# The second query-key product over all 128 rows of TensorE, with a zero-padded query tile

## The chip, the cores and the metric

One NeuronCore of a Trainium2 chip runs the whole program. The metric is the device time of one launch in microseconds (us), lower is better. TensorE does the matmuls (PE in the profile, with PEld for its weight loads), VectorE is DVE, ScalarE is ACT, GpSimd is POOL, and SP issues the DMAs. A matmul here takes a weight tile of at most 128 rows (the contracted dimension, on the partitions) by 128 columns, and streams up to 512 columns of the other operand past it into a bank of PSUM.

## What is computed

One inference step of a single transformer layer for 1024 prompt tokens and 64 sample tokens, width 1024, all in fp32. Cut to what matters here:

```python
h = pre(x, g_pre_mix, shift1, scale1)                  # RMSNorm, then conditioning
qd, kd, vd, qs, ks, vs = split_proj(h @ w_in)
# 4 heads of differential attention, two maps of 64 features each
s = einsum('bqhmd,bkhmd->bhmqk', qd, kd) * 64 ** -0.5 - slopes * dist
p = softmax(where(visible, s, NEG)); a = p[:, :, 0] - lam * p[:, :, 1]
od = rmsnorm(a @ vd) * (1 - lam_init)
# 8 heads of stick-breaking attention of 64 features each
z = einsum('bqhd,bkhd->bhqk', qs, ks) * 64 ** -0.5
w = where(earlier, exp(log_sigmoid(z) + between), 0); osb = w @ vs
x = x + gate1 * rmsnorm(concat(od, osb) @ w_out)
x = x + gate2 * rmsnorm(relu(h2 @ w_up) ** 2 @ w_down)
```

The sample's 64 queries attend to 1024 cached keys and their own 64.

## The kernel before

TensorE reads a reduced fp32 form, so every operand is held as an exact sum of a high and a low part (`split`), and a product is the sum of three partial products, high-high, high-low and low-high.

**Stages.** Up to about 55 us the conditioning vectors and the first tokens are prepared. From there to about 745 us attention runs, with the input projections of the eight units mixed in. Then come the output projection (to about 820 us) and the feed-forward part, a long row of matmuls (lines 299 to 301 and 1117 to 1120) up to the end.

**Units and steps.** There are eight units `u`: 0 to 3 are the differential heads, 4 to 7 are pairs of stick-breaking heads. A unit has two halves of 64 features, its two maps or its two heads, on partitions 0 to 63 and 64 to 127. The class `Diff` makes a step of one query tile `t` of 128 queries and both maps; `Stick` makes a step of two query tiles, 2q and 2q + 1, and one head `hd`; `Sample` is the sample's step. Each step has a `score` part (query-key products and the weights from them), an `apply` part (the weights transposed on TensorE, line 572, and multiplied with the values, lines 588 and 589 or 737 and 738) and a `finish` part. The main loop runs `apply` of step j and `score` of step j + 1 alternately, and between them the `Filler` puts pieces of the next unit's projections (lines 299 to 301), so many per piece of attention that each token group is done when a step needs it: the list `need` holds these due steps.

**The product that is touched.** `qk` (line 557) makes one block of up to 512 scores in two matmuls into one PSUM bank. Per half `m`, the tile `Q[m]` holds the high part of the queries on the half's own 64 partitions and the low part on the other 64, and `Kd[m]` holds the high part of the keys twice. So line 561 contracts over 128 rows and gives high-high plus low-high in one go. Line 562 adds the queries' high part times the keys' low part `Kl`; it contracts over the half's 64 rows only:

```python
mm(ps[:, :w], lhsT=S["Q"][m][:, qt], rhs=S["Kd"][m][:, c0 : c0 + w], start=True, stop=False)
mm(ps[:, :w], lhsT=S["Q"][m][r, qt], rhs=S["Kl"][r, c0 : c0 + w], start=False, stop=True)
```

A `Diff` step's scores go to DVE (line 641, minimum) and ACT (line 610, exponential), a `Stick` step's to ACT (lines 716 and 717, two sigmoids), POOL (line 701, the triangular mask) and DVE (lines 693 and 694, running product and weights).

**Order and buffers.** The order on each engine comes from the framework's scheduler, which starts from the order in which the code is written. Each engine takes its instructions strictly in that order. Tiles of one tag share a fixed number of buffers: tag `h` (6 buffers) holds the projections' input parts, later those of the output projection and of the feed-forward part, and at the end the tiles `xy` of the last sums.

Of the kernel before, what the change touches and what calls it, by code (L numbers as in the profile page):

```python
# [34 lines left out]
def build(tc, I, O):  # L35
# [9 lines left out]
    BUFS = dict(h=6, w=6, raw=3, qk=10, v=2, s=11)  # L45
# [16 lines left out]
    def split(src, hi, lo, eh=None, el=None):  # L62
        """src = hi + lo exactly, both in FP32r."""
        (eh or nc.scalar.copy)(hi, src)  # L64
        (el or nc.vector).tensor_tensor(lo, src, fr(hi), ALU.subtract)  # L65
# [4 lines left out]
    # ------------------------------------------------------------- constants  # L70
# [21 lines left out]
    # ---------------------------------------------------------------- x load  # L92
# [9 lines left out]

    def group_tiles(name):
        return [[big(f"{name}{c}{g}", "h", [P, KT, 384]) for c in "hl"] for g in range(3)]
# [11 lines left out]
    # conditioning vectors, gains and biases of adaLN: rows to be transposed into columns  # L116
# [64 lines left out]
    # --------------------------------------------------------- adaLN columns  # L181
    gD = dr.tile([2, 2, D], F32, name="gD")

    def ada_rows(c0, name, ps=None, between=()):
        """silu(c) @ w_ada for 256 columns from c0, prompt's and sample's in rows 32j and 32j + 1: four summands in TensorE's four
        column tiles, the rows between them 0."""
        if ps is None:
            ps = bank("pa" + name, "pj")[:, :256]
        for q in range(2):
            raw = ada_raws.get((c0, q))  # L190
            if raw is None:
                raw = big(f"ar{name}{q}", "raw", [P, 4, 256], F32)
                load(raw, w_ada[:, 4 * q : 4 * q + 4, c0 : c0 + 256])
            if q == 1 and between:
                between.pop()()
            for i in range(4):
                mm(ps[32 * i : 32 * i + 32], lhsT=sc[:, 4 * q + i, :], rhs=raw[:, i, :], start=(q == 0), stop=(q == 1), skip_group_check=True)
            yield 0.5
        return ps

    def sum_to_columns(R, n, name):
        """Rows' summands added, features on the partitions: [128, feature block, prompt | sample]."""
        ps = bank(name, "pj")
        for i in range(n):
            mm(ps[:, 2 * i : 2 * i + 2], lhsT=R[:, i * P : (i + 1) * P], rhs=sel, start=True, stop=True)
        return ps[:, 0 : 2 * n].rearrange("p (k j) -> p k j", j=2)

    def modulation(first, cols, name):
        """Columns A = (1 + scale) * gain and B = shift."""
# [21 lines left out]
    def gate_rows(first, gpost, name, slot, tags):  # L231
        """(gate + bias) * gain by conditioning vector, to DRAM."""
# [22 lines left out]
    def split_T(x, half, dst, m, rows):  # L255
        """Half of the token tile's transposed rows into its group's parts; the sample's also side by side (hi | lo)."""
# [7 lines left out]
    def modulated(ps, half, m, A, B, dst, name):  # L264
        """One half of the features, from the transposed normalised rows to the group's parts."""
# [28 lines left out]
    def dense_T(ps, w, act, g, ks=range(KT)):  # L294
        """ps[128 output features, the group's tokens]; yields its cost by and by."""
# [19 lines left out]
    def columns(ps, q):  # L315
        """Columns 2q, 2q+1 of A = (1 + scale) * gain and B = shift, from rows [shift | scale]."""
# [9 lines left out]
    def block_T(g, k, tag):  # L326
        """Feature block k of the group's normalised tokens, features on the partitions."""
# [25 lines left out]
    def first(k):  # L353
        """Block k's part of the first group's products."""
        for i in range(3):
            drain(dense_T(PS[i], PW[0, i], hT, 0, (k,)))
# [46 lines left out]
    # lambda  # L403
# [11 lines left out]
    # per row: 1 for the first map's queries, -lambda for the second's  # L415
# [4 lines left out]
    # ---------------------------------------------------------- projections  # L420
# [6 lines left out]
    for i in range(2):  # L427
        nc.scalar.copy(bd[:, i, :], zero)

# [8 lines left out]
    def natural(f, u, g, out, name):  # L438
        """Tokens back onto partitions, and to the output."""
# [91 lines left out]
    def proj(u, g):  # L531
        for i, f in enumerate((proj_q, proj_k, proj_v)):
            if (u, i) not in PW:
                PW[u, i] = proj_weights(u, i)
            for n, c in enumerate(f(u, g, PW[u, i])):
                yield c
                # the next group gets ready meanwhile
# [14 lines left out]

    # --------------------------------------------- attention, step by step
    # A step has parts `score` (products with the keys, and the weights from them), `apply` (weights transposed, times the
    # values) and `finish` (to the mixed features); `finish` and the next step's `score` run between parts of `apply`.

    def qk(u, m, t, c0, w, name):
        S = U[u]
        ps = bank(name, "qk")
        r, qt = slice(64 * m, 64 * m + 64), slice(P * t, P * t + P)  # L560
        mm(ps[:, :w], lhsT=S["Q"][m][:, qt], rhs=S["Kd"][m][:, c0 : c0 + w], start=True, stop=False)  # L561
        mm(ps[:, :w], lhsT=S["Q"][m][r, qt], rhs=S["Kl"][r, c0 : c0 + w], start=False, stop=True)  # L562
# [5 lines left out]
    def transposed(srcs, name, kr=P):  # L568
        """[rows, 128] blocks to [128, rows] side by side, in two parts."""
# [8 lines left out]
    def apply_rows(po, parts, values):  # L578
        """Weights' rows on output partitions: po[rows, value hi | lo] over blocks of (group, its weights' sources, rows)."""
# [27 lines left out]
    def exp_rows(e, mn, l):  # L607
        """e = exp(-e + mn) per chunk, their sum in l[:, 0:1]."""
# [12 lines left out]
    class Diff:  # L621
        def __init__(self, u, t):
            self.u, self.t, self.name = u, t, f"{u}_{t}"
            self.cost = 0.33 * (t + 1) + 0.8 * (1 + t // 4) + 0.1

# [60 lines left out]
    def stick(s, kp):  # L686
        """Chunks in place: kp = sigmoid(-z) becomes its product over this and all later keys, s = sigmoid(z) the weights
        (the very last key's s is 0 in every row)."""
# [9 lines left out]
    def earlier(s, kp, n):  # L698
        """Only keys before the query: [rows, n] with row and key counted from the same position."""
# [3 lines left out]
    class Stick:  # L703
        def __init__(self, u, q, hd):
            self.u, self.q, self.hd, self.name = u, q, hd, f"{u}_{q}{hd}"
            self.cost = 0.22 * (4 * q + 3) + 0.43 * (q + 1) + 0.1

# [56 lines left out]
    # the sample's: queries of two maps (or heads) on the partitions, keys of the cache and then the new ones  # L764
# [4 lines left out]
    class Sample:  # L769
        def __init__(self, u):  # L770
            self.u, self.name, self.cost = u, f"S{u}", 6.3

# [112 lines left out]
    class Filler:  # L885
        """Work for TensorE between the steps' dependent parts."""
# [35 lines left out]
    def merge(a, b):  # L922
        """a's parts with b's between them."""
# [22 lines left out]
    for u in range(8):  # L946
        sec = [st for st in sections[u] if not isinstance(st, Sample)]
        for st, g in zip((sec[0], sec[3], sec[6]) if u < 4 else (sec[0], sec[2], sec[6]), range(3)):
# [10 lines left out]
    def some(rows, n):  # L959
        """The next n chunks of adaLN's rows."""  # L960
# [9 lines left out]
    for u in range(8):  # L970
        for g in range(3):
            if u + g:
                fill.add(proj(u, g), 12, (u, g))
            if g == (2) and u in others:
                gen, n, c = others[u]
                fill.add(some(gen, n), c, "end" if u == 7 else None)
    drain(steps[0].score())
    prev = None
    for j, st in enumerate(steps):
# [4 lines left out]
        ratio = max([fill.cost_to(mark) / sum(cost[j : i - 1]) for i, mark in need if i > j + 1 and sum(cost[j : i - 1]) > 0] + [0.0])  # L984
        for c in merge(st.apply(), nxt.score() if nxt is not None else ()):
# [8 lines left out]
    # ------------------------------------------------------------ out_proj  # L994
# [18 lines left out]
    def tail_T(m, xn):  # L1013
        g = m // 3
        if h2[g] is None:
            h2[g] = [big(f"h2{c}{g}", "h", [P, KT, 384]) for c in "hl"]
        modulated_T(xn, m, A2, B2, h2, f"b{m}")

    for m in range(NTT):
# [24 lines left out]
        # x' = x + gate * gain * rmsnorm, and its rows over their root mean square  # L1044
# [13 lines left out]
    # ---------------------------------------------------------------- FFN  # L1058
# [49 lines left out]
    def down(b, m, blocks, then=None):  # L1108
        """Adds hidden blocks (parts of the hidden tiles, weights) to the token tile's sum."""
# [21 lines left out]
    def last_down(b, m, blocks, G):  # L1131
        """The token tile's last blocks, then out = x + G * rmsnorm(sum)."""
# [76 lines left out]
def constants():  # L1209
    """Arrays that depend on shapes alone: ALiBi distances with the chunk mask, and selectors."""  # L1210
# [31 lines left out]
```

## Time and profile before

| | us |
|---|---|
| median of 3 runs | 1632.2 (1627.46 to 1635.94) |
| profiled execution, first to last instruction (its own time is not listed apart from this span) | 1633.9 |
| up to the first scores | 55 |
| differential units, settled | 120 to 400 |
| stick-breaking units | 400 to 680 |
| last unit's attention, its projections done | 680 to 745 |
| output projection | 745 to 820 |
| feed-forward part | 820 to 1634 |

Of the views, the page gives the busy time of each engine over the whole span, and the chain of work that ended last: from the last instruction back to what released it, step by step, so that an engine's share of the chain is the share of the span that it set. A matmul's record runs from its start to a modelled end, and successive matmuls overlap; what one costs in a row of matmuls is the distance from its start to the next one's start. A weight load that begins while the matmul before still runs is hidden. The windows view gives busy times for stretches of the span, with the granted clock of TensorE as a share of 2.4 GHz.

### The profile page before, as it was taken

The page shows a single profiled execution, that of the slowest core. Times are in us where ns is not written, and L with a number is a line of the kernel's source. Part 1 is how long each engine was busy: PE and PEld are TensorE (multiplying, and loading weights), DVE is VectorE, ACT ScalarE, POOL GpSimd, SP SyncE. Part 2 cuts the span into 40 slices and gives each one's busy share as a digit, 9 for nine tenths or more (in the row PEclk, how much of TensorE's full clock was granted, in tenths as well). Part 3 has the DMA queues.
Part 4 walks back from the last instruction along what each step waited for, and adds up shares of the span by engine and source line. Part 5 has one row for each costly group of instructions (what it writes and reads, how often), then busy time and mean ns, then how long its engine had stood idle before and what let it go on. Part 6 is the DMA issues. An engine that isn't in the chain of part 4 may idle for free.

```text
span 1633.9 us, 23611 instructions
## 1 busy us (share of the span) xinstructions
PE 1582.2 (97%) x8682; PEld 1364.0 (83%) x8682; DVE 981.2 (60%) x1880; ACT 707.2 (43%) x1661; POOL 330.3 (20%) x516
## 2 busy tenths in 40 slices
PE   6999999999999999978999999999999999999998
PEld 4779887878797988757889899889989989998996
DVE  3675667676878788797554344454454455445447
ACT  3756666666655656664665312122111212211122
POOL 0442333333433242253211000000000000000002
PEclk9799999999998999778999999999999999999999
DMA  9312124232313120346321201222111111111124
GB/s 320 87 49 86 59 80 119 82 113 74 113 50 114 47 87 20 95 133 205 128 80 60 75 19 62 78 79 62 41 32 47 40 52 52 51 40 34 45 90 161
DMA packets 152517, 133.21 MB, mean 82 GB/s; under 512 B 11233, under 2 KB 136274, under 8 KB 152402
## 3 DMA queue, kind: packets, MB, share of 16 engines
q1 hardware_dynamic: 152402, 131.71, 25.9%
q8 instruction: 68, 1.11, 0.3%
q14 instruction: 47, 0.39, 0.1%
HBM read 108.59 MB, written 23.09 MB: 81 GB/s over the span
## 4 chain that ended last, share of the span: by engine, by line
PE 83%; DVE 7%; issue 3%; ACT 1%; POOL 1%; DMA 1%; POOLq 0%; DVEq 0%; ACTq 0%
PE pu L300 8%; PE pu L299 8%; PE pu L301 8%; PE pd L1117 7%; PE pd L1118 7%; PE pd L1120 6%; PE pz L562 4%; PE pt L572 2%; PE pz L561 2%; DVE k L693 2%; PE pq L299 2%; PE py L1032 2%; PE pk L299 2%; PE py L1031 2%; PE pq L300 2%
## 5 line engine op out<-in xcount | busy, mean ns | idle before, releaser
L1124 DVE TENSOR_TENSOR acc<-pd,acc 128x512 f32<-128x512 f32 x252 | 171.0, 687 | 112.2 <-PE pd L1120 105.9
L1102 ACT ACTIVATE sq<-pu 128x384 f32<-128x384 f32 (+1 forms) x96 | 45.3, 472 | 315.1 <-PE pu L301 315.1
L1103 DVE TENSOR_TENSOR sq<-sq 128x384 f32<-128x384 f32 (+1 forms) x96 | 72.0, 750 | 178.4 <-ACT sq L1102 178.4
L562 PE MATMUL pz<-Kl,Q 64*128 64x512 f32 (+2 forms) x192 | 88.9, 463 | 0.0
L65 DVE TENSOR_TENSOR al<-pt,ah 128x512 fp32r<-128x512 f32 (+2 forms) x128 | 75.8, 599 | 19.7 <-ACT ah L64 18.1
L64 ACT CAST ah<-pt 128x512 fp32r<-128x512 f32 (+2 forms) x128 | 65.0, 521 | 39.2 <-PE pt L572 29.6
L561 PE MATMUL pz<-K,Q 128*128 128x512 f32 (+2 forms) x192 | 77.8, 406 | 2.1 <-ACT K L498 1.2
L572 PE MATMUL pt<-ident,s 128*128 128x128 f32 x432 | 74.1, 289 | 3.1 <-DVE s L663 2.6
L610 ACT ACTIVATE s<-s,mn 128x512 f32<-128x512 f32 (+3 forms) x96 | 58.5, 611 | 37.1 <-DVE mn L641 34.8
L562 PEld LDWEIGHTS pz<-Kl,Q 64*128 64x128 f32 x192 | 37.1, 193 | 42.6 <-issue 36.8
L693 DVE TENSOR_TENSOR_SCAN k<-k 128x127 f32<-128x127 f32 (+3 forms) x64 | 56.0, 878 | 13.3 <-POOL k L701 12.6
L716 ACT ACTIVATE s<-pz 128x512 f32<-128x512 f32 (+2 forms) x96 | 47.5, 495 | 34.4 <-PE pz L562 25.2
L694 DVE TENSOR_TENSOR s<-s,k 128x127 f32<-128x127 f32 (+3 forms) x96 | 60.6, 634 | 1.3
L572 PEld LDWEIGHTS pt<-ident,s 128*128 128x128 f32 x432 | 52.2, 147 | 8.4 <-issue 3.6
L65 DVE TENSOR_TENSOR rl<-sq,rh 128x384 fp32r<-128x384 f32 x64 | 35.7, 558 | 35.6 <-ACT rh L64 35.4
L701 POOL TENSOR_SCALAR_AFFINE_SELECT s<-s 128x128 f32<-128x128 f32 x64 | 27.6, 432 | 112.2 <-ACT s L716 111.9
L64 ACT CAST rh<-sq 128x384 fp32r<-128x384 f32 x64 | 32.9, 514 | 40.1 <-DVE sq L1103 38.1
L561 PEld LDWEIGHTS pz<-K,Q 128*128 128x128 f32 x192 | 38.9, 203 | 13.6 <-issue 4.4
L717 ACT ACTIVATE k<-pz 128x512 f32<-128x512 f32 (+2 forms) x96 | 47.4, 494 | 6.0 <-DVE k L693 3.0
L641 DVE CUSTOM_DVE_ANT_0 s<-pz,T 128x512 f32<-128x512 f32 (+3 forms) x64 | 37.6, 588 | 20.0 <-PE pz L562 19.1
L738 PE MATMUL po<-al,V 128*128 128x256 f32 (+1 forms) x160 | 45.3, 316 | 4.4 <-DVE al L65 4.4
L737 PE MATMUL po<-ah,V 128*128 128x256 f32 (+1 forms) x160 | 47.7, 306 | 0.8 <-ACT ah L64 0.8
(1225 smaller groups left out, 5182.0 us busy)
## 6 DMA issues: line engine op xcount, KB each, us to landing
arr<-in_w_ada SPq DMA_DIRECT2D x16, 512.0 KB, 3.5
arm<-in_w_ada SPq DMA_DIRECT2D x16, 512.0 KB, 4.8
ar<-in_w_ada SPq DMA_DIRECT2D x10, 512.0 KB, 4.7
mixD<-mx SPq DMA_DIRECT2D x32, 128.0 KB, 1.7
xr<-in_x_prompt SPq DMA_DIRECT2D x16, 256.0 KB, 4.0
xD<-xr SPq DMA_DIRECT2D x16, 256.0 KB, 4.2
xy<-xD SPq DMA_DIRECT2D x8, 512.0 KB, 4.6
out_y_prompt<-xy SPq DMA_DIRECT2D x16, 256.0 KB, 2.1
```

Of the source, the lines that this page charges most:

```text
L64: (eh or nc.scalar.copy)(hi, src)
L65: (el or nc.vector).tensor_tensor(lo, src, fr(hi), ALU.subtract)
L299: mm(ps[:, :n], lhsT=wh[:, k, :], rhs=hh[:, k, :n], start=(k == 0), stop=False)
L300: mm(ps[:, :n], lhsT=wh[:, k, :], rhs=hl[:, k, :n], start=False, stop=False)
L301: mm(ps[:, :n], lhsT=wl[:, k, :], rhs=hh[:, k, :n], start=False, stop=(k == 7))
L561: mm(ps[:, :w], lhsT=S["Q"][m][:, qt], rhs=S["Kd"][m][:, c0 : c0 + w], start=True, stop=False)
L562: mm(ps[:, :w], lhsT=S["Q"][m][r, qt], rhs=S["Kl"][r, c0 : c0 + w], start=False, stop=True)
L572: nc.tensor.transpose(pt[:kr, i * P : (i + 1) * P], a, ident)
L1117: mm(ps, lhsT=rh[:, off : off + P], rhs=wh[:, cols], start=(j == 0), stop=False)
L1118: mm(ps, lhsT=rh[:, off : off + P], rhs=wl[:, cols], start=False, stop=(m == 8 and end))
L1120: mm(ps, lhsT=rl[:, off : off + P], rhs=wh[:, cols], start=False, stop=end)
L1124: nc.vector.tensor_tensor(acc[m][:, cols], ps, acc[m][:, cols], ALU.add)
```

## The change

1. Line 562 contracts over all 128 rows. Its weight tile is no longer the half's 64 rows of `Q[m]` but a column block of a new tile `QZ[m]` (128 x 256, one buffer per half), in which the other half's 64 rows are zero. `Kl` is read with all its 128 rows; the other half's keys meet zeros.
2. `QZ` is zeroed once by four ACT copies. After that a POOL copy of 64 x 256 (`pad_queries`) writes the queries' high part of two neighbouring query tiles: for both maps before each even `Diff` step, for its head before each `Stick` step. A new method `ready` does this; the main loop calls it for step j + 1 just before `apply` of step j and `score` of step j + 1. There are 64 such copies. As there is one buffer, a copy has to wait until TensorE has read the pair before, and TensorE's first line-562 matmul of a step has to wait for the copy.
3. A copy for tiles t and t + 1 reads the queries of both, so in units 0 to 3 the second token group is due one step earlier (`need`).
4. The room for `QZ` comes from the tag `h`: it has 5 buffers, and the low part of the third token group has one of its own (`hs`), 320 columns wide instead of 384.

Line 562 of before is line 576 of the changed kernel, line 561 is 575, and the copy is line 442.

```diff
-    BUFS = dict(h=6, w=6, raw=3, qk=10, v=2, s=11)
+    BUFS = dict(h=5, hs=1, w=6, raw=3, qk=10, v=2, s=11)
...
+    def pair(name, g):
+        return [big(f"{name}{c}{g}", *(("hs", [P, KT, 320]) if (c, g) == ("l", 2) else ("h", [P, KT, 384]))) for c in "hl"]
...
+    QZ = [sb.tile([P, 2 * P], F32R, name=f"qz{m}") for m in range(2)]
+    for m in range(2):
+        for i in range(2):
+            nc.scalar.copy(QZ[m][:, i * P : (i + 1) * P], zero)
+
+    def pad_queries(u, m, t):
+        r = slice(64 * m, 64 * m + 64)
+        nc.gpsimd.tensor_copy(QZ[m][r], fr(U[u]["Q"][m][r, P * t : P * t + 2 * P]))
...
-        r, qt = slice(64 * m, 64 * m + 64), slice(P * t, P * t + P)
+        qt = slice(P * t, P * t + P)
         mm(ps[:, :w], lhsT=S["Q"][m][:, qt], rhs=S["Kd"][m][:, c0 : c0 + w], start=True, stop=False)
-        mm(ps[:, :w], lhsT=S["Q"][m][r, qt], rhs=S["Kl"][r, c0 : c0 + w], start=False, stop=True)
+        mm(ps[:, :w], lhsT=QZ[m][:, (t % 2) * P : (t % 2 + 1) * P], rhs=S["Kl"][:, c0 : c0 + w], start=False, stop=True)
...
+        def ready(self):
+            if self.t % 2 == 0:
+                for m in range(2):
+                    pad_queries(self.u, m, self.t)
...
+        def ready(self):
+            pad_queries(self.u, self.hd, 2 * self.q)
...
-        for st, g in zip((sec[0], sec[3], sec[6]) if u < 4 else (sec[0], sec[2], sec[6]), range(3)):
+        for st, g in zip((sec[0], sec[2], sec[6]), range(3)):
...
+    steps[0].ready()
     drain(steps[0].score())
...
+        if nxt is not None:
+            nxt.ready()
         for c in merge(st.apply(), nxt.score() if nxt is not None else ()):
...
-            h2[g] = [big(f"h2{c}{g}", "h", [P, KT, 384]) for c in "hl"]
+            h2[g] = pair("h2", g)
```

The scheduler's order moves with it. Two places show how.

On TensorE, in unit 2, from the scores of query tile 3 to those of tile 4 (names `pz_<tile><map><chunk>`). Before:

```order
L561 MATMUL pz_300_3047<-K_2307,Q_2233 128x512
L562 MATMUL pz_300_3047<-Kl_2309,Q_2233 128x512
L616 MATMUL pm_7_2826<-ident,od_7_2671 128x128
L561 MATMUL pz_310_3083<-K_2308,Q_2234 128x512
L562 MATMUL pz_310_3083<-Kl_2309,Q_2234 128x512
L572 MATMUL pt_10_2970<-ident,s_10_0_2840 128x128 x2
```

The same place now:

```order
L575 MATMUL pz_300_3107<-K_2314,Q_2208 128x512
L576 MATMUL pz_300_3107<-Kl_2316,qz_493 128x512
L303 MATMUL pv_3059<-h1h_119,wv2h 128x320
L304 MATMUL pv_3059<-h1l_120,wv2h 128x320
L305 MATMUL pv_3059<-h1h_119,wv2l 128x320
L575 MATMUL pz_310_3124<-K_2315,Q_2209 128x512
L576 MATMUL pz_310_3124<-Kl_2316,qz_494 128x512
L586 MATMUL pt_10_3008<-ident,s_10_0_2885 128x128 x2
L630 MATMUL pm_7_2871<-ident,od_7_2719 128x128
L575 MATMUL pz_400_3204<-K_2314,Q_2208 128x512
L576 MATMUL pz_400_3204<-Kl_2316,qz_493 128x512
```

Tile 4's first scores have moved up close behind tile 3's, and both read the one buffer `qz_493`, so the copy has to fit between the second row and the last.

On POOL at the same point of the program (`od`, `rsd`: the normalisation at the end of a `Diff` step; `wk3l`: a weight's low part). Before:

```order
L674 TENSOR_SCALAR od_7_2671<-od_7_2671,rsd_7_2677 128x128
L65 TENSOR_TENSOR wq3l<-wq3r,wq3h 128x1024
L65 TENSOR_TENSOR wk3l<-wk3r,wk3h 128x1024
L80 TENSOR_SCALAR rsd_0_2792<-ssd_0_2790,le_0_2784 128x1
L81 TENSOR_TENSOR rsd_0_2792<-rsd_0_2792,mhalf 128x1
```

Now:

```order
L693 TENSOR_SCALAR od_7_2719<-od_7_2719,rsd_7_2725 128x128
L65 TENSOR_TENSOR wk3l<-wk3r,wk3h 128x1024
L442 CAST qz_493<-Q_2208 64x256
L442 CAST qz_494<-Q_2209 64x256
L65 TENSOR_TENSOR wv3l<-wv3r,wv3h 128x1024
L80 TENSOR_SCALAR rsd_0_2828<-ssd_0_2826,le_0_2820 128x1
```

The two copies have been put between rows of other work, behind a weight's low part and ahead of the next step's normalisation.

## Rows read from the trace of the kernel before

**Rows 1.** Page: engines' busy us; chain by line; a DMA group, us to landing.

```profile
PE 1582.2 (97%) x8682; PEld 1364.0 (83%) x8682; DVE 981.2 (60%) x1880; ACT 707.2 (43%) x1661; POOL 330.3 (20%) x516
...
PE pu L300 8%; PE pu L299 8%; PE pu L301 8%; PE pd L1117 7%; PE pd L1118 7%; PE pd L1120 6%; PE pz L562 4%; PE pt L572 2%; PE pz L561 2%; DVE k L693 2%; PE pq L299 2%; PE py L1032 2%; PE pk L299 2%; PE py L1031 2%; PE pq L300 2%
...
xy<-xD SPq DMA_DIRECT2D x8, 512.0 KB, 4.6
```

**Rows 2.** Windows view: busy us (instructions) by engine, granted clock, DMA.

```profile
core 0: us, PE busy (x) PEld busy (x) DVE busy (x) ACT busy (x) POOL busy (x), PEclk, DMA share, GB/s
55.00:120.00 65.00, 61.69 (x278) 48.47 (x277) 42.55 (x120) 41.34 (x109) 27.55 (x35) 0.83 0.11 32
120.00:400.00 280.00, 276.21 (x1684) 234.48 (x1683) 183.99 (x529) 174.74 (x510) 91.65 (x150) 1.00 0.30 89
400.00:680.00 280.00, 273.92 (x1652) 230.62 (x1650) 228.74 (x383) 174.54 (x409) 95.29 (x167) 0.95 0.26 76
680.00:745.00 65.00, 50.97 (x235) 37.50 (x235) 56.05 (x79) 37.97 (x80) 32.00 (x35) 0.71 0.33 103
```

**Rows 3.** Line 562: count and forms; its windows (PE, PEld, clock).

```profile
L562 PE MATMUL pz<-Kl,Q x192: 322/492/793, 55.3 to 726.7; 64*128 64x512 f32 x96, 64*128 64x128 f32 x32, 64*128 64x256 f32 x32, 64*128 64x384 f32 x32
...
120.00:400.00 280.00, 34.89 (x80) 14.61 (x80) 1.00 0.30 89
400.00:680.00 280.00, 35.53 (x78) 14.87 (x78) 0.95 0.26 76
```

**Rows 4.** Timeline from 408 us: start, duration, instruction [idle before].

```profile
408.18 0.40 PE L561 MATMUL pz<-K,Q 128*128 128x512 f32 x1
408.51 0.18 PEld L562 LDWEIGHTS pz<-Kl,Q 64*128 64x128 f32 x1 [0.28 <-issue]
408.51 0.50 PE L562 MATMUL pz<-Kl,Q 64*128 64x512 f32 x1
...
408.94 0.19 PEld L299 LDWEIGHTS pk<-h1h,wk4h 128*128 128x128 f32 x1 [0.25 <-issue]
...
408.94 0.41 PE L299 MATMUL pk<-h1h,wk4h 128*128 128x320 f32 x1
...
409.19 0.31 PE L300 MATMUL pk<-h1l,wk4h 128*128 128x320 f32 x1
...
409.33 0.31 PE L301 MATMUL pk<-h1h,wk4l 128*128 128x320 f32 x1
```

**Rows 5.** Timeline from 474.8 us: two of the sample's products, 128 rows.

```profile
474.82 0.39 PE L811 MATMUL pzS<-ckh,bd 128*128 128x512 f32 x1
...
475.05 0.40 PE L812 MATMUL pzS<-ckl,bd 128*128 128x512 f32 x1
```

**Rows 6.** Chain of waits by line, 120 to 400 us, then 400 to 680.

```profile
by line: PE pz L562 10.1%; PE po L588 7.5%; PE pk L299 6.0%; PE pv L299 6.0%; PE pq L299 6.0%; PE pv L301 5.7%; PE pk L301 5.6%; PE pk L300 5.6%; PE pz L561 5.6%; PE pv L300 5.5%; PE pq L301 5.4%; PE pq L300 5.4%; PE pt L572 4.5%; PE po L58
...
by line: issue 10.4%; PE pz L562 7.1%; PE pt L572 6.7%; DVE k L693 6.4%; PE pq L299 4.4%; PE pz L561 4.1%; PE pk L299 4.0%; PE pq L301 3.9%; PE pq L300 3.8%; PE po L738 3.7%; PE pk L300 3.7%; PE po L737 3.4%; PE pk L301 3.3%; PE pv L300 3.0
```

**Rows 7.** Groups on POOL: busy us, mean ns | idle before.

```profile
L701 POOL TENSOR_SCALAR_AFFINE_SELECT k<-k 128x128 f32<-128x128 f32 x64 | 25.6, 399 | 18.1 <-ACT k L717 17.3
...
L65 POOL TENSOR_TENSOR h1l<-xt,h1h 128x320 fp32r<-128x320 f32 x8 | 7.5, 943 | 11.7 <-ACT h1h L64 11.7
...
L65 POOL TENSOR_TENSOR wk4l<-wk4r,wk4h 128x1024 fp32r<-128x1024 f32 x1 | 2.4, 2410 | 0.0
```

**Rows 8.** Waits of DVE, 400 to 680 us: total us, times, longest.

```profile
DVE k L693 <- POOL k L701: 10.2, 17, 1.4
DVE al L65 <- ACT ah L64: 9.8, 10, 2.2
DVE mx L757 <- ACT ot L756: 7.1, 7, 3.8
DVE skt L693 <- POOL skt L701: 5.0, 3, 2.2
DVE Kl L499 <- ACT K L498: 4.7, 7, 1.8
```

More of the change, by code (lines that the diff above doesn't have):

```diff
@@ L101, in load_halves @@
             load(t[:rows], src[:, 512 * i : 512 * i + 512])
+    def pair(name, g):
+        return [big(f"{name}{c}{g}", *(("hs", [P, KT, 320]) if (c, g) == ("l", 2) else ("h", [P, KT, 384]))) for c in "hl"]
     def group_tiles(name):
-        return [[big(f"{name}{c}{g}", "h", [P, KT, 384]) for c in "hl"] for g in range(3)]
+        return [pair(name, g) for g in range(3)]
     def load_halves(tiles, src, rows):
@@ L771, in __init__, with ready @@
             self.u, self.name, self.cost = u, f"S{u}", 6.3
+        def ready(self):
+            pass
         def cache(self):
```

## The prediction

> **What bounds the kernel now.** I read the page first: TensorE is busy 97% of the span and the matmul lines fill the chain; line 562, the instruction that the change touches, has 4% of it, line 561 with the same count and columns only 2% [rows 1]. The feed-forward part is not touched, so I went to the windows of attention, then to the chain inside them, then to the timeline around one pair.
>
> The windows [rows 2] show four kinds of stretch. From 120 to 400 us (differential units) TensorE is busy 276 of 280 us at full clock, DVE 184, ACT 175: TensorE sets the pace. From 400 to 680 (stick-breaking units) it is busy 274, but DVE has 229, and the granted clock is 0.95: a second engine is close behind. From 680 to 745 DVE has 56 of 65 us and the clock is 0.71: DVE sets the pace. From 55 to 120 work starts up, at 0.83. Line 562 has 192 matmuls, half of them 512 columns wide, 384 on average; 80 lie in the second stretch, 78 in the third, 34 outside the two [rows 3].
>
> The chain says how many of them matter. It spends 10.1% of 280 us = 28.3 us on line 562 in the differential stretch and 7.1% = 19.9 us in the stick-breaking one, where "issue" (10.4%) and DVE lines have a good part [rows 6].
>
> **What one 64-row matmul costs.** This is the core of the sum, read from the timeline [rows 4]. Starts: line 561 at 408.18, line 562 at 408.51, the next matmul (L299, 320 columns) at 408.94, the one after at 409.19, then 409.33. The last distance, 0.14 us, is the usual one for 320 columns; for 512 columns and 128 rows it is 0.23 (474.82 to 475.05) [rows 5]. So three matmuls that would take 0.23 + 0.23 + 0.14 = 0.60 us take 1.01. The reason stands in the weight loads: line 562's begins at 408.51, together with its matmul and after 0.28 us of idle time, and the next 128-row load likewise at 408.94, after 0.25 us; neither is hidden beneath the matmul before it. The 64-row matmul is cut off on both sides, and the price does not hang on its width: **0.41 us each**, 192 x 0.41 = 79 us if all were on the path.
>
> [...]
>
> **The change part by part.**
>
> *Line 562 over 128 rows.* On the chain a line-562 piece is its normal distance, 384/512 x 0.23 = 0.17 us, plus the 0.20 by which its own step is too long (0.43 - 0.23 [rows 4, 5]): 0.37 us. So 28.3 / 0.37 = 76 of 80 lie on the chain in the differential stretch and 19.9 / 0.37 = 54 of 78 in the stick-breaking one. Ceilings: 76 x 0.41 = 31 us and 54 x 0.41 = 22 us. The other 34: 14 us.
>
> What is late next? In the differential stretch, if 280 us become 249, DVE's 184 are 74% and ACT's 175 are 70%: nothing steps in, and I take 30 us. In the stick-breaking stretch DVE has 228.7 us of work and waits 36.8 us for ACT and POOL in its five longest kinds of wait (10.2 + 9.8 + 7.1 + 5.0 + 4.7 [rows 8]). If these stay, the stretch can't fall below 265.5 us: 14.5 us of gain against a ceiling of 22. Some of ACT's lateness itself comes from TensorE, so this floor may give a little; I take 14. Of the 34 others I take 6 of 14 us, since from 680 us on DVE is the bound. Sum: **50 us**.
>
> *The 64 POOL copies.* No row shows a one-input POOL copy of 64 x 256. From below: the mask on 128 columns takes 0.40 us; from above: a two-input operation on 320 columns takes 0.94 [rows 7]. It has one input, like the mask, and 256 columns; I take 0.7, so 45 us of POOL work, on an engine that is busy 92 of 280 us and 95 of 280 [rows 2]. A gain is excluded: the copy adds work and takes none away. On the path it counts only where TensorE waits for it. All but the first two copies overwrite tiles that TensorE has to read first: 62 handovers. In the new order, all but two of these have 22 or more TensorE rows between the last read of the old queries and the first of the new ones, at 0.14 us some 3.1 us; the two copies of a Diff step take 1.4. The two closest have 8 and 9 rows, some 1.3 us, and behind a weight's low part of 2.4 us [rows 7] they would cost 0.7 + 2.4 - 1.3 = 1.8 us each: 4 us. Queued behind a copy on POOL are the next masks, for which DVE's running products wait (10.2 us already [rows 8]); a copy mostly falls where POOL waits anyway, and I add 2 us. Together **6 us** lost; bounds 0 and 62 x 0.94 = 58.
>
> *The due step of the second token group.* It moves projection matmuls earlier and adds none. Where TensorE has filler work to choose from, that costs nothing; in the start-up stretch, where TensorE is idle 65 - 61.7 = 3.3 us [rows 2], it may cost or bring these 3.3. I take 0.
>
> *Buffers and zeroing.* Five `h` buffers instead of six matter only at the end, where the sums' tiles `xy` are loaded. A load lands after 4.6 us [rows 1] and a token tile's last 24 matmuls take 24 x 0.23 = 5.5 us, so four tiles in flight instead of five are enough: 0. Without that cover each of the four or five loads that now have to wait for a buffer would cost up to 4.6 us. The four zeroing copies run on ACT before its first data are there: 0.
>
> **Sum:** 30 + 14 + 6 - 6 = 44 us. The profiled span is 1633.9, 1.7 us above the median of the runs and inside their spread, so I put the sum on it without correction: 1633.9 - 44 = **1590 us**.
>
> **The rivals.**
>
> *The stick-breaking stretch keeps its length and the clock falls.* DVE gives the pace there as soon as TensorE is faster, and TensorE then stands idle between bursts. For it: DVE's 229 of 280 us, and a clock of 0.95, that is 28 us at 1.2 GHz, in the stretch where DVE lines and "issue" are on the chain, against 1.00 where TensorE never stops [rows 2, 6]. If nothing is gained there, and as much again (28 us) runs at half clock, half of which is on the path with a doubled distance, 7 us go back: 30 + 0 + 4 - 6 - 7 = 21 us, 1613. Against it: 54 of the 78 matmuls are on the chain there now.
>
> *The whole ceiling.* All of 31 + 22 us, 10 of the 14 outside, and handovers that cost 2: 61 us, 1573. Against it: DVE would then be busy 229 of 258 us, with waits in between as today.
>
> *Nothing.* The full-height load is not hidden here although lines 811 and 812 show it hidden, because its tile is written by POOL just before: only the copies' 2 to 6 us are left, 1638. [...] Against it: by [rows 5] two 128-row matmuls in the same bank follow each other without loss.
>
> *Slower: TensorE waits at the handovers.* Place: the first line-562 matmul of a step, with everything behind it in TensorE's strict order. POOL works in order too, so a copy can stand behind a normalisation or a mask that waits for ACT, or one of six behind a weight's low part of 2.4 us. It decides from 50 / 62 = 0.8 us of wait per handover on; with 1.5 us each the time is 1633.9 - 50 + 93 = 1677. Against it: 3.1 us of cover at 60 of 62.
>
> **How the numbers follow.** Forecast 0.70 (1590, with its own spread 1577 to 1607), the stretch that keeps its length 0.14 (1613), the ceiling 0.08 (1573), nothing 0.03 (1638), slower 0.05 (1677). The range takes in the forecast, most of the ceiling case and the first rival: 1570 to 1614. A measurement here can tell about 0.5%, 8 us, from no change: faster 0.70 + 0.08 + 0.13 = 0.91, same 0.01 + 0.03 = 0.04, slower 0.05.
>
> **What would show it.** Line 576 should be 128 rows high, its weight loads starting inside the matmul before, with starts 0.23 us apart for 512 columns, and its share of the chain should fall to that of line 575 or below. The stretch of the differential units should shorten by about 30 us with TensorE still at full clock and without waits for POOL; the stick-breaking one by about 14, with DVE lines up in the chain. The feed-forward part should keep its length. I am wrong if TensorE's waits list `qz` from POOL with more than some 10 us, if the clock in the stick-breaking stretch falls well below 0.95, or if line 576's load still starts only with its matmul.

## The result and the profile after

The changed kernel takes 1586.97 us in the median of four runs (1580.62 to 1589.99), the kernel before beside it 1632.66: a ratio of **0.9715 [0.9686, 0.9744]**, 46 us less. Run again beside other kernels it gave 0.9754 [0.9727, 0.9782]. The forecast was 1590, in a range of 1570 to 1614. The profiled execution took 1589.58 us, with a span of 1587.9. The total came out as forecast; the terms did not, as the experiments show.

From the page of the changed kernel, the answers to [rows 1]: busy time by engine, the chain by engine and line, and three groups (busy us, mean ns of one | idle time of the engine before them, what ended it).

```profile
PE 1517.0 (96%) x8682; PEld 1357.9 (86%) x8682; DVE 987.2 (62%) x1880; ACT 703.3 (44%) x1665; POOL 366.7 (23%) x580
...
PE 74%; DVE 12%; issue 4%; ACT 3%; DMA 2%; POOL 1%; SPq 0%; POOLq 0%; DVEq 0%; ACTq 0%
PE pu L303 8%; PE pu L304 8%; PE pu L305 8%; PE pd L1145 8%; PE pd L1146 8%; PE pd L1148 7%; DVE k L712 4%; PE py L1059 2%; PE py L1060 2%; PE pt L586 2%; DVE s L713 2%; PE py L1062 2%; PE pq L304 1%; PE pq L303 1%; PE pq L305 1%
...
L575 PE MATMUL pz<-K,Q 128*128 128x512 f32 (+2 forms) x192 | 74.8, 393 | 6.4 <-ACT k L739 2.2
...
L576 PE MATMUL pz<-Kl,qz 128*128 128x512 f32 (+2 forms) x192 | 69.8, 369 | 0.0
...
L442 POOL CAST qz<-Q 64x256 fp32r<-64x256 f32 x64 | 34.7, 542 | 66.3 <-PE pz L576 63.9
```

The second product has left the list of the chain, where line 562 had 4%; DVE line 713 has come in, and line 712 (693 before) has gone from 2% to 4%. The copies cost 542 ns in the mean, and POOL stands 63.9 us waiting for TensorE's last reading of the old pair; e2 below shows what that costs.

The timeline of TensorE and its weight loads around one pair, the counterpart of [rows 4]:

```profile
495.57 0.34 PE L305 MATMUL pk<-h1h,wk6l 128*128 128x384 f32 x1
495.57 0.19 PEld L575 LDWEIGHTS pz<-K,Q 128*128 128x128 f32 x1
495.75 0.40 PE L575 MATMUL pz<-K,Q 128*128 128x512 f32 x1
495.75 0.19 PEld L576 LDWEIGHTS pz<-Kl,qz 128*128 128x128 f32 x1
495.98 0.39 PE L576 MATMUL pz<-Kl,qz 128*128 128x512 f32 x1
495.98 0.19 PEld L303 LDWEIGHTS pk<-h1h,wk6h 128*128 128x128 f32 x1
496.21 0.34 PE L303 MATMUL pk<-h1h,wk6h 128*128 128x384 f32 x1
```

Line 576's load starts with line 575's matmul, at 495.75, and is over before its own matmul starts at 495.98; the next load begins at 495.98 and is hidden too. The starts are 0.23 us apart, where [rows 4] had 0.33 and 0.43. So weight loads of 128 rows ran under matmuls of 128 rows here.

The windows, against [rows 2] (the same borders in time, though the work has moved forward against them):

```profile
core 0: us, PE busy (x) PEld busy (x) DVE busy (x) ACT busy (x) POOL busy (x), PEclk, DMA share, GB/s
55.00:120.00 65.00, 59.06 (x347) 52.16 (x348) 46.85 (x131) 44.77 (x123) 33.53 (x45) 0.97 0.15 45
120.00:400.00 280.00, 269.30 (x1756) 247.38 (x1754) 201.15 (x552) 185.95 (x539) 120.84 (x196) 0.96 0.31 91
400.00:680.00 280.00, 258.59 (x1706) 237.72 (x1698) 248.28 (x413) 182.16 (x431) 112.71 (x200) 0.94 0.30 86
680.00:745.00 65.00, 57.11 (x265) 46.67 (x264) 52.12 (x78) 38.26 (x83) 25.02 (x26) 0.90 0.59 190
```

TensorE does more matmuls in each stretch and yet stands idle more in the two long ones: 10.7 of 280 us in the differential stretch (3.8 before), 21.4 in the stick-breaking one (6.1 before). The two are not quite alike: before, the record of a 64-row matmul (0.50 us) covered its whole step of 0.43 us [rows 4], so that the time cut off was booked as busy.

By stages, from the starts of the second products and of the feed-forward part: the first second product comes 4.9 us later than before (60.3 against 55.3); unit 0 takes 14.2 us less (83.5 to 69.3), units 1 to 3 take 14.3 less (250.5 to 236.2), units 4 to 7 take 20.3 less up to the last second product (337.3 to 317.0), and the way from there to the feed-forward part takes 3.1 less: 47 us.

**An account of TensorE's time.** From the traces I worked out one sum for every kernel, up to the first matmul of the feed-forward part. From the distance between each matmul's start and the next I took its columns / 2.4 in ns, plus 14 ns: at full clock 128-row matmuls of 320, 384 and 512 columns among others of 128 rows start 147, 174 and 229 ns apart in the median (before). As measured, the 2.4 and 1.2 GHz above are these 2.4 columns a ns and, at the lower level, 1.2. What is left is put down as: "cut off" where one of the two, or the matmul before, has fewer than 128 rows (up to 0.4 us each); "half clock" where the trace gives the granted clock as 0.50, the only other level in the traces of before and of the changed kernel (the same three distances are then 267, 320 and 427 ns; a cut-off that falls there stands here too, and not under "cut off"); "waits" where it is 0.15 us or more; "small" for the rest. The work itself is 634 us (635 in e7) in all of them.

| kernel | cut off | waits | half clock | small | feed-forward starts |
|---|---|---|---|---|---|
| before | 80.9 | 47.4 | 57.6 | 32.0 | 854.4 |
| changed | 12.3 | 75.9 | 44.1 | 38.3 | 807.5 |
| e1, 64 rows | 86.1 | 51.4 | 64.6 | 32.6 | 871.4 |
| e4, 128 rows in differential units only | 48.3 | 53.3 | 55.1 | 33.2 | 826.6 |
| e2, no copies | 10.5 | 77.5 | 41.7 | 40.9 | 807.2 |
| e3, due step only | 85.1 | 52.2 | 60.5 | 29.2 | 863.6 |
| e5, old due step | 10.0 | 88.6 | 45.1 | 40.9 | 821.4 |
| e6, buffers only | 86.8 | 55.8 | 35.7 | 31.8 | 847.0 |
| e7, two short products for one | 87.0 | 48.2 | 56.0 | 28.9 | 858.3 |
| e9, height only | 10.8 | 94.8 | 36.8 | 40.5 | 819.7 |
| e10, height and due step | 10.9 | 78.6 | 45.2 | 40.7 | 811.9 |
| e11, changed, less DVE work | 11.4 | 67.0 | 32.8 | 42.2 | 790.2 |
| e12, before, less DVE work | 88.8 | 42.3 | 19.5 | 33.3 | 820.6 |

Changed against before: 68.6 us of cut-off gone (0.36 us for each of the 192; some 20 of them fall at half clock, and over the others it is 0.40), 28.5 us of new waits, 13.5 less at half clock, 6.3 more in small pieces: 47 us.

Every row is one execution, and how a piece is divided between the columns is a choice. How far a row can be trusted is seen from before and e6, whose medians agree within 0.1%: they differ by 22 us in half clock, 8 in waits and 6 in cut-off (e6 has other buffers, and so perhaps another order). The fall of cut-off by some 70 us is far beyond that; differences of 10 us in one of the other columns are not.

### The profile page after: what moved, and what is told of

It is laid out like the page before. It is cut to its first block, busy times and chain, and to the rows that moved or that the text cites. A ratio compares the mean times of both kernels' runs of the same rounds, so it can differ in the third digit from the quotient of the medians.

```text
span 1587.9 us, 23684 instructions
## 1 busy us (share of the span) xinstructions
PE 1517.0 (96%) x8682; PEld 1357.9 (86%) x8682; DVE 987.2 (62%) x1880; ACT 703.3 (44%) x1665; POOL 366.7 (23%) x580
## 4 chain that ended last, share of the span: by engine, by line
PE 74%; DVE 12%; issue 4%; ACT 3%; DMA 2%; POOL 1%; SPq 0%; POOLq 0%; DVEq 0%; ACTq 0%
PE pu L303 8%; PE pu L304 8%; PE pu L305 8%; PE pd L1145 8%; PE pd L1146 8%; PE pd L1148 7%; DVE k L712 4%; PE py L1059 2%; PE py L1060 2%; PE pt L586 2%; DVE s L713 2%; PE py L1062 2%; PE pq L304 1%; PE pq L303 1%; PE pq L305 1%
## 5 line engine op out<-in xcount | busy, mean ns | idle before, releaser
L1130 ACT ACTIVATE sq<-pu 128x384 f32<-128x384 f32 (+1 forms) x96 | 45.2, 471 | 310.8 <-PE pu L305 310.8
L576 PE MATMUL pz<-Kl,qz 128*128 128x512 f32 (+2 forms) x192 | 69.8, 369 | 0.0
L712 DVE TENSOR_TENSOR_SCAN k<-k 128x127 f32<-128x127 f32 (+3 forms) x64 | 62.1, 980 | 4.3 <-POOL k L720 4.0
L713 DVE TENSOR_TENSOR s<-s,k 128x383 f32<-128x383 f32 (+3 forms) x96 | 62.9, 662 | 1.4
L65 DVE TENSOR_TENSOR rl<-sq,rh 128x384 fp32r<-128x384 f32 x64 | 35.7, 558 | 37.9 <-ACT rh L64 37.9
L575 PEld LDWEIGHTS pz<-K,Q 128*128 128x128 f32 x192 | 38.3, 200 | 15.1 <-ACT k L739 4.5
L442 POOL CAST qz<-Q 64x256 fp32r<-64x256 f32 x64 | 34.7, 542 | 66.3 <-PE pz L576 63.9
L660 DVE CUSTOM_DVE_ANT_0 s<-pz,T 128x512 f32<-128x512 f32 (+3 forms) x64 | 37.2, 585 | 10.8 <-PE pz L576 10.3
```

Of the source, the lines that this page charges most:

```text
L712: nc.vector.tensor_tensor_scan(k, k, k, 1.0 if c == n - 1 else kp[c + 1][:, 0:1], ALU.mult, ALU.bypass)
```

## The experiments

**The height undone (e1).** Everything of the change stays but the rows:

```diff
-        qt = slice(P * t, P * t + P)
+        r, qt = slice(64 * m, 64 * m + 64), slice(P * t, P * t + P)
...
-        mm(ps[:, :w], lhsT=QZ[m][:, (t % 2) * P : (t % 2 + 1) * P], rhs=S["Kl"][:, c0 : c0 + w], start=False, stop=True)
+        mm(ps[:, :w], lhsT=QZ[m][r, (t % 2) * P : (t % 2 + 1) * P], rhs=S["Kl"][r, c0 : c0 + w], start=False, stop=True)
```

> The changed kernel with only the height of the second product undone: it reads its 64 rows of the padded tile and of the keys' low part; copies, buffers and due steps stay. Theory (the switch of height between matmuls is what the change saves, 192 times): the whole gain of 46 us goes, the copies stay as a cost of at most some 5 us: 1628 to 1640 us, second-product starts again cut off on both sides. Rival A (the gain comes from the new order, the earlier due step or the clock at the opening): 1587 to 1600. Rival B (a mixture): in between, and the place in between gives the share.

Measured: 1649.96 us, 1.0122 [1.0088, 1.0157]. The gain goes, as the theory has it, and more, so that the time lies above its band: at 64 rows the rest of the change is a loss of 20 us, four times the 5 expected. The weight loads of the second product start late again (behind the last bar: us idle before them, and the part that the view puts down to "issue"); first the kernel before, then e1:

```profile
L562 PEld LDWEIGHTS pz<-Kl,Q 64*128 64x128 f32 x192 | 37.1, 193 | 42.6 <-issue 36.8
```
```profile
L576 PEld LDWEIGHTS pz<-Kl,qz 64*128 64x128 f32 x192 | 36.9, 192 | 41.1 <-issue 32.4
```

In the changed kernel the waits name no such idle time for line 576. On top of the rest of the change, the height is worth 1.0122 - 0.9754 = 3.7% or 60 us (66 with the first ratio, 64 between the profiled spans).

**The differential units alone (e4).** The same edit as in e1, with `r` all 128 rows where `u < 4`.

> The changed kernel with 128 rows in the differential units only; the 96 second products of the stick-breaking units read their 64 rows of the padded tile. Theory (every switch costs about the same on the path in both kinds of unit, 46 us over 192 matmuls): half the gain is left, 1606 to 1614 us. Rival (the prediction's split, 30 in the settled differential stretch and 14 behind it, since DVE bounds the stick-breaking stretch): 1597 to 1604.

Measured: 1604.13 us, 0.9840 [0.9801, 0.9879]. That lies between the two bands, at the upper edge of the rival's; the trace tells more. Against e1 the feed-forward part starts 45 us earlier: 38 us of cut-off are gone, waits grow by 2 only, and half clock falls by 9.5, which is within what rows of one kernel differ by. From there to the changed kernel, the stick-breaking units: 36 us of cut-off gone as well, but waits up by 23, and 19 us are left. So equal savings, one kept whole, the other kept by half.

**The copies left out (e2).** The line with `nc.gpsimd.tensor_copy(QZ[m][r], ...)` is taken out.

> The changed kernel without the 64 POOL copies: the padded tile stays zero, so the second product adds nothing to the scores (the keys' low part is left out of them), at the same height, widths and count. Theory (the handovers cost TensorE nothing, as the trace shows no wait for them): 1582 to 1592 us, as the changed kernel. Rival (the prediction's 6 us, or the 28 us of ceiling that came back as waits, belong to copies and handovers): 1560 to 1581.

Measured: 1590.55 us, 0.9759 [0.9720, 0.9799], as with the copies (0.9754 when run again). The copies and handovers cost nothing that can be measured. In the changed kernel's waits between 55 and 700 us line 576 never waits for a copy; TensorE meets one once, for 0.4 us, at the weight load of another product, while POOL waits 63.9 us for TensorE (waits view: total us, times, longest):

```profile
PEld pmS L630 <- POOL qz L442: 0.4, 1, 0.4
```
```profile
POOL qz L442 <- PE pz L576: 63.9, 35, 5.0
```

**The due step alone (e3)**, in the kernel before:

```diff
-        for st, g in zip((sec[0], sec[3], sec[6]) if u < 4 else (sec[0], sec[2], sec[6]), range(3)):
+        for st, g in zip((sec[0], sec[2], sec[6]), range(3)):
```

> The kernel before with the earlier due step of the second token group alone, 64 rows in the second product, no padded tile, no copies. Theory: no change, 1628 to 1640 us. Rival (the opening and unit 0, where 14 us were gained and the half clock went from 22 to 3 us, gained by the earlier projections and not by the height): 1612 to 1625.

Measured: 1639.49 us, 1.0060 [1.0038, 1.0083], 10 us slower. By its number it lies within the theory's band, but the interval does not hold 1: at 64 rows the earlier due step costs, and explains half of e1's 20 us.

**The due step put back (e5)**, in the changed kernel. `need` takes the old list, and tiles 2 and 3 of a differential unit are copied singly:

```diff
-            if self.t % 2 == 0:
+            if self.t % 2 == 0 or self.t == 3:
                 for m in range(2):
-                    pad_queries(self.u, m, self.t)
+                    pad_queries(self.u, m, self.t, 1 if self.t in (2, 3) else 2)
```

> The changed kernel with the due step of the second token group put back to the fourth step of a differential unit. Tiles 2 and 3, which lie in different token groups, are copied one at a time for that (128 columns each), so there are 80 copies instead of 64; the rest is as in the changed kernel. Theory (the earlier due step cost the 64-row kernel 10 us and costs the 128-row kernel as much): 1574 to 1581 us. Rival (its cost came from the particular order of the 64-row kernel only): 1584 to 1592.

Measured: 1604.91 us, 0.9861 [0.9827, 0.9895], 17 us slower than with the earlier step. Both expectations fall: at 128 rows the earlier due step gains. The account puts 12.7 us of the difference down as waits, not much more than its rows differ by themselves. The 16 more copies are in this number too, though e2 gives copies no price.

**The buffers alone (e6)**, in the kernel before: `h=5, hs=1` and `pair`, as in the change's diff.

> The kernel before with the buffers of the changed one alone: five of tag h and one of tag hs, 64 rows, no copies, old due step. The changed kernel at 64 rows was 20 us slower than before and the due step alone 10 us, so some 10 us are open. Theory (buffers cost nothing, as the prediction said; the 10 us are the copies and their handovers): 1626 to 1634 us. Rival (the buffers cost it, by an input part of the third token group that has to wait): 1635 to 1643.

Measured: 1629.24 us, 1.0010 [0.9990, 1.0031]. No price, as predicted. The other 10 us of e1 are neither buffers nor waits for copies (line 576 waits 0.9 us for them in e1, three times); by elimination they belong to the order that the scheduler makes with the copies in it, which no run showed directly. That the copies keep other work on POOL waiting at 64 rows is not excluded either.

**Two short products for one (e7)**, in the kernel before:

```diff
+        n = 2 if w == 512 else 1
+        for c in range(0, w, w // n):
-        mm(ps[:, :w], lhsT=S["Q"][m][r, qt], rhs=S["Kl"][r, c0 : c0 + w], start=False, stop=True)
+            mm(ps[:, c : c + w // n], lhsT=S["Q"][m][r, qt], rhs=S["Kl"][r, c0 + c : c0 + c + w // n], start=False, stop=(c + w // n == w), skip_group_check=True)
```

> The kernel before with each of the 96 second products of 512 columns as two 64-row matmuls of 256 columns, nearly all of them side by side. Theory (the price is paid where the height changes, 128 to 64 and back, and a second 64-row matmul behind the first adds little): 96 more matmuls at some 0.04 us, 1630 to 1642 us. Rival (each 64-row matmul pays by itself, 0.2 us or more): 1650 to 1670.

Measured: 1639.51 us, 1.0057 [1.0027, 1.0087]: 96 more matmuls for 9 us. The timeline shows a pair of halves (x2 stands for both):

```profile
133.87 0.40 PE L561 MATMUL pz<-K,Q 128*128 128x512 f32 x1
134.19 0.29 PEld L564 LDWEIGHTS pz<-Kl,Q 64*128 64x128 f32 x2 [0.31 <-issue]
134.19 0.50 PE L564 MATMUL pz<-Kl,Q 64*128 64x256 f32 x2
134.62 0.19 PEld L301 LDWEIGHTS pv<-h1h,wv1l 128*128 128x128 f32 x1
134.63 0.45 PE L301 MATMUL pv<-h1h,wv1l 128*128 128x384 f32 x1
...
134.91 0.39 PE L561 MATMUL pz<-K,Q 128*128 128x512 f32 x1
```

From the first half's start to the next 128-row matmul it is 0.44 us (134.19 to 134.63); one whole 64-row matmul took 0.43 [rows 4]. Over the 79 pairs at full clock the median is 0.430 us, over the 86 whole ones of the kernel before 0.428. The second one was all but free: the price was paid once on the way from 128 to 64 rows and back, not per matmul. So the 9 us are not 96 times the price of a second matmul. Ten of the 96 products have their halves apart, with other matmuls between them, and so switch once more, which at the account's 0.40 us each is an estimate of some 4 us; where the rest comes from is open.

**The height alone (e9), and with the due step (e10)**, in the kernel before, without padded tile, copies or buffers:

```diff
-        mm(ps[:, :w], lhsT=S["Q"][m][r, qt], rhs=S["Kl"][r, c0 : c0 + w], start=False, stop=True)
+        mm(ps[:, :w], lhsT=S["Q"][m][:, qt], rhs=S["Kl"][:, c0 : c0 + w], start=False, stop=True)
```

> The kernel before with the height alone: the second product takes as weights the same 128 rows of the query tile as the first one and all 128 rows of the keys' low part; no padded tile, no copies, old buffers, old due step. The other half's rows add the product of two low parts, which the kernel before leaves out. Theory (the height alone is worth what the changed kernel gains over its own 64-row form, 64 us, and the rest of the change only moved the order): 1560 to 1576 us, faster than the changed kernel. Rival (the rest of the change is needed for the gain): 1584 us or more.

> The same with the earlier due step of the second token group. Theory (the due step costs 10 us, as it did at 64 rows): 10 us slower than without it, 1570 to 1586 us. Rival (the sign of a moved due step hangs on the rest of the order, as the 16 us that putting it back cost the changed kernel suggest): equal to the version without it or faster.

The rows that are added multiply the low part of this half's queries with the low part of the other half's keys, a small term that belongs to no score.

Measured: e9 1602.08 us, 0.9820 [0.9792, 0.9848]; e10 1592.69 us, 0.9768 [0.9728, 0.9808]. The theory for e9 falls: alone, the height brings 29 us and not 64, though the same cut-off is gone (80.9 to 10.8). 47 us come back as waits. The waits of TensorE in e9 between 60 and 800 us, then in the changed kernel from 60 to 830, whose longest kinds are shorter:

```profile
PE po L738 <- DVE al L65: 9.3, 7, 4.6
PE pz L561 <- ACT k L717: 5.8, 6, 2.4
PE poS L589 <- DVE alS L65: 4.9, 2, 2.6
PE pz L561 <- DVE smn L829: 3.5, 2, 2.1
PE pt L572 <- DVE al L65: 3.5, 2, 3.3
PE pm L616 <- POOL od L674: 3.4, 3, 2.7
PE par L197 <- DMA arr<-in_w_ada: 3.3, 3, 1.6
```
```profile
PE po L760 <- DVE al L65: 6.6, 7, 2.0
PE poS L603 <- DVE alS L65: 4.0, 3, 1.9
PE par L201 <- DMA arr<-in_w_ada: 3.7, 5, 1.6
PE ptS L586 <- DVE ss L713: 2.8, 1, 2.8
PE pt L586 <- DVE s L713: 2.6, 2, 2.4
```

No single wait carries it; they are many, for several engines. In e10, the earlier due step shortens the waits from 94.8 to 78.6 us, as in the changed kernel (88.6 in e5 to 75.9), and the time by 9 us. The two intervals overlap, but e5 and the changed kernel show the same sign. e10 is within the error of the changed kernel without any copy; none of the versions that do the whole work is faster than it.

**Less work for DVE (e11 in the changed kernel, e12 in the kernel before).**

```diff
-            nc.vector.tensor_tensor(s[c][:, : w - 1], s[c][:, : w - 1], kp[c][:, 1:w], ALU.mult)
+            nc.vector.tensor_tensor(s[c][:, :32], s[c][:, :32], kp[c][:, 1:33], ALU.mult)
```

> The changed kernel with DVE relieved in the stick-breaking units: the multiplication of weights and running products covers 32 columns of each chunk instead of all (the weights beyond them are left unmultiplied), which takes some 50 us off DVE's 278 us between 366 and 683 us; every dependency stays. Theory (behind the height, DVE is the next bound in the stick-breaking units): the time falls by 12 us or more, to 1576 or below. Rival (TensorE still sets the pace there, and the waits come from the order): a fall of less than 8 us.

> The same relief in the kernel before. Theory (with 64 rows TensorE sets the pace and DVE matters less): the time falls by clearly less than in the changed kernel, 0 to 10 us, to 1620 or above. Rival (DVE weighs the same in both): the same fall as in the changed kernel.

Measured: e11 1570.45 us, 0.9644 [0.9607, 0.9680], 18 us less than the changed kernel; e12 1603.63 us, 0.9846 [0.9818, 0.9875], 25 us less than before. In the windows below the edit takes 37 and 39 us off DVE, not 50. So DVE's work counts in the stick-breaking units, but at 64 rows no less than at 128: the theory, that it became the bound through the change, falls, though e11 by itself lies in its band. The windows from the first second product of unit 4 to the last one of all, in before, e12, the changed kernel and e11:

```profile
389.00:727.00 338.00, 327.72 (x1916) 271.24 (x1914) 273.92 (x464) 211.95 (x499) 117.16 (x205) 0.92 0.26 77
```
```profile
384.00:695.00 311.00, 307.13 (x1910) 255.26 (x1910) 234.71 (x460) 208.77 (x496) 95.07 (x201) 1.00 0.28 82
```
```profile
366.00:683.00 317.00, 291.85 (x1900) 267.49 (x1900) 277.95 (x460) 208.10 (x496) 139.73 (x238) 0.92 0.28 82
```
```profile
362.00:661.00 299.00, 281.64 (x1900) 256.61 (x1899) 241.41 (x457) 205.48 (x492) 117.39 (x234) 0.97 0.28 84
```

Before, the relief took the granted clock from 0.92 to 1.00: 0.08 x 338 = 27 us, which is all that was gained (338 to 311). That is one execution of each; over the whole span, all four of e12 were granted 0.988 to 0.990 and the seven of before beside them 0.971 to 0.978, which in the medians makes 19 of the 24 us. In the changed kernel it went from 0.92 to 0.97 in this stretch, and TensorE stays idle for 17 of 299 us although DVE has 58 us to spare. So with DVE relieved the height is worth 12 us in this stretch, without relief 21: something other than DVE's amount of work holds the changed kernel there.

**The changed kernel again (e8)**, unaltered.

> The changed kernel once more, unaltered, beside the others of this call: 1580 to 1590 us, ratio 0.970 to 0.975.

Measured: 1588.82 us, 0.9754 [0.9727, 0.9782]. The ratio is 0.0004 above the band; the two measurements of the changed kernel differ by 0.4%, the size of an interval here.

## Why the prediction came out right, point by point

- **The price of one 64-row matmul** (0.41 us, 79 us for all): the mechanism held, and the size too: 0.36 to 0.40 us each in the account. That the price does not hang on the width was read from one pair of 512 columns; it holds: at full clock the two steps around a line-562 matmul are too long by 0.27, 0.33, 0.29 and 0.32 us in the median at 128, 256, 384 and 512 columns (the step behind them, which the prediction counted too, is not in this). e7 puts the price where the prediction read it, on the two sides of the matmul.
- **What of it lies on the path**: the term that was off. The chain's share gave ceilings of 31 and 22 us, of which 30 and 14 were taken, and 6 for the rest: 50. With all else of the change in place, e1 and e4 give 45 us for the differential units and 19 for the others: 64. The term of 30 for the settled differential units is met: from e1 to e4 units 1 to 3 shorten by 29.6 us (265.1 to 235.5). What was too small is the 6 for "the other 34", which held the opening: unit 0 alone shortens by 14.7 us there (84.6 to 69.9). Part of that is the granted clock, which was in no term and differs between executions: e12, whose code is that of before in unit 0, took 78.2 us for it where before took 83.5 (granted clock from 55 to 130 us: 0.93 in e12, 0.85 in before; 0.86 in e1 and 0.94 in e4). Set directly against the kernel before, units 1 to 3 gain 14.3 us and not 30, since at 64 rows the rest of the change makes them 14.6 us longer (250.5 to 265.1).
- **The stick-breaking term** (14 of 22): right in kind, since half the saving comes back as waits, but the reason given, DVE's floor of 265.5 us, is not what the runs show. In the changed kernel the chain from 400 to 680 us does go through DVE, as forecast:

```profile
by line: DVE k L712 17.6%; DVE s L713 8.6%; DVE al L65 5.9%; issue 4.3%; PE pt L586 3.9%; PE pq L303 2.8%; PE po L760 2.7%; PE pq L304 2.6%; PE pq L305 2.6%; DVE sk L712 2.5%; PE pz L575 2.4%; PE pz L576 2.1%; PE po L759 2.1%; ACT k L739 2.
```

  but e11 and e12 show that DVE's work weighed as much before. A share of the chain told which engine is in it, not that it caps the gain.
- **Handovers and copies** (6 us lost): nothing measurable was lost. A copy takes 0.395 us in the median, as the lower of the two bounds, 0.40 [rows 7], and 0.54 in the mean, not the 0.7 taken; the two close handovers priced at 1.8 us each, like all the others, never made line 576 wait.
- **The due step** (0, within 3.3): wrong, in size and in where it acts. It cost 10 us at 64 rows and gained 9 (e9 to e10) to 17 (e5 to the changed kernel) at 128. The 3.3 us were the idle time of the opening; that the moved projections act through the order of what stands behind them is the likely reason, and not shown.
- **Buffers, zeroing, feed-forward** (0): right. e6 is at 1.001, and from its first matmul to the end the feed-forward part takes 779.5 us before and 780.4 after.
- **The rivals**: the stick-breaking stretch did not keep its length (338 to 317 us), and its clock stayed at 0.92. "Nothing" and the handovers were wrong, by the load hidden at 495.75 and by waits for copies that line 576 does not have. "The whole ceiling" is nearest in its mechanism: nearly all the cut-off went, but 28.5 us came back as waits.
- **The total**: 44 us were forecast and 46 came. That it fits so closely is luck. With the other parts first, two errors of opposite sign meet: the height gives 60 to 66 and not 50, the rest of the change takes 20 and not 6. With the height first it is 29, then 9 by the due step, then some 2 to 9 by the rest. The parts do not add; what is fixed is the cut-off of some 70 us, and what returns as waits differs with the rest of the code (47 us in e9, 28.5 in the changed kernel). That the order decides it is the likely reading; no run changed the order alone.

Two things stay open: why the earlier due step has the other sign at 128 rows, and which dependence holds TensorE in the stick-breaking units once DVE is relieved. Neither was settled.

## What to carry to other kernels

A matmul of 64 rows between matmuls of 128 cost the hiding of a weight load on either side here, 0.36 to 0.40 us each in the account, and at every width from 128 to 512 (0.27 to 0.33 us in the two steps around it alone): fill up the rows with zeros, or with rows whose product is small enough to be left in, as in e9, or put short matmuls side by side. Find such places in the timeline by weight loads that start together with their matmul, as at 408.51 [rows 4]. Of the saving, count on what the chain says only for a fixed order: where a scheduler makes a new order, a local gain of 70 us came out as anything from 29 to 66, so cost the order as a term of its own, with a range of some 15 us to both sides here, and not as zero.

## What the runs showed of the hardware

- The switch of height had the price, not the height: 0.430 us in the median for two 64-row matmuls of 256 columns side by side (e7), 0.428 for one of 512 (before), from the first start to the next 128-row matmul's.
- 128-row weight loads ran under 128-row matmuls: loads of 0.19 us that start at 495.75 and 495.98 are over before the matmuls at 495.98 and 496.21 (changed kernel).
- With less work on DVE the granted clock of TensorE was higher: with 64 rows 1.00 in the stick-breaking stretch (e12, TensorE idle for 4 of 311 us) instead of 0.92 (before, idle for 10 of 338), one execution each; over the whole span 0.988 to 0.990 in four executions instead of 0.971 to 0.978 in seven. The time lost to the lower level, 0.08 x 338 = 27 us of this stretch in the execution before, was more than the idle time of 10 us.
